# A fused two-block transformer kernel: the dense gates' layout in DRAM

## The chip, the cores and the metric

The kernel runs as one program on one core of a Trainium2 chip. The metric is the device time of the program in microseconds, as the median of several runs. The core has five engines that are named by their letters here: PE (matrix multiplication), DVE (VectorE), ACT (ScalarE), POOL (GpSimd) and SP (which issues DMAs). Sixteen DMA engines move data between DRAM and on-chip memory; they take their work from queues. In this kernel q1 is the queue of the transfers that SP issues, and q0 the queue of the gathers that POOL issues.

## The reference

One sequence of 512 tokens with 1024 features in float32 passes through two blocks. The first has a convolution branch, a windowed attention branch and then PEER, a layer with 16,384 small experts; the second has a linear recurrence, a sliding attention and a cross attention. The change is in PEER:

```
sc = einsum('thpd,pnd->thpn', q, sub_keys)      # 8 heads x 2 halves x 128 keys
vals, idx = top_k(sc, 16)
cand = vals[:, :, 0, :, None] + vals[:, :, 1, None, :]
top_s, pos = top_k(cand, 16)                     # 16 experts per head, 128 per token
gate = softmax(top_s)
u = expert_u[expert_idx];  act = gelu(einsum('thkd,td->thk', u, hc))
out = einsum('thk,thkd->td', gate * act, expert_v[expert_idx])
```

An expert's number is 128 i + j, with key i of the first half and key j of the second.

## The kernel before

The kernel handles the four tiles of 128 tokens in two ways. The two tiles of the front (`dense = 2`, 256 tokens) go through all 16,384 experts as dense matrix products, with a gate of zero where an expert was not chosen. The two other tiles fetch only their chosen experts, a row of u and v of 8 KB per token and expert: 256 gathers of 128 rows (1 MB each), issued by POOL (line 193) into six slots of `uv`. For each gather DVE makes a dot product with the token's row (L220), ACT the gelu and the scaling (L222, L223), and DVE adds the scaled v to x (L231); only then is the next gather issued. Both ways run at the same time.

The dense way has two stages. In `route` the gate matrix is built. For each block of 16 tokens (`sub`, eight per tile, so 16 in all) DVE, POOL and ACT make one-hot matrices A and B (L734, L737, L745), PE multiplies them (L747) and ACT copies the result into `cs`, 128 partitions (key i) by 128 keys j by 16 tokens, 1 MB (L749). SP writes cs into the DRAM tensor `gates` (L753). `cs` has two buffers. Beside this PE already computes the first 32 values of j of the expert activations (`expert_in`, L835 loads a tile of u of 512 KB, L837 multiplies, L839 applies gelu). The tiles of u lie in six buffers.

In `experts` the loop runs over 16 groups of eight keys j. For each group SP loads `cg`, the gates of these eight keys for all 256 tokens, 1 MB in two buffers (L853). For each pair of keys DVE multiplies the activations by cg in place (L860). Then some steps of the gathered way are put in: the remaining gathers (POOL issues 232 from 875 us on) are spread evenly over the 64 pairs, so 3 or 4 per pair. SP loads the two tiles of v (L865, 512 KB each, four buffers), PE multiplies (L869, 16 matmuls) and adds up in four banks, and `expert_in` is called for the pair that is 16 pairs later. Its result goes into the slot of `acts` that the present pair has just left, so that DVE can be at most 16 pairs ahead of PE.

The order on each engine is fixed when the program is built: a scheduler puts the instructions in order by priority and by its own costs, and the engines then wait for one another by semaphores. All loads and stores by SP leave in one order in one queue, so v and u stand behind cg where cg was issued first. A read of `gates` waits until all writes into it that it needs have landed; since each group needs all 16 blocks, the first cg waits for the last write.

In DRAM `gates` has the form [16 blocks, 128 partitions, 128 keys x 16 tokens]. A write of one block is 8 KB in a row for each partition. A read of a group takes, for each partition, 16 pieces of 512 bytes that lie 1 MB apart.

Of the kernel before, what the change touches and what calls it, by code (L numbers as in the profile page):

```python
# [8 lines left out]
F32 = mybir.dt.float32  # L9
# [231 lines left out]
class Kern:  # L241
    ahead = 32
    dense = 2
    slots = 6
    near = 6
    low = False
    wide = False

# [403 lines left out]
    def peer(self, x, h, xp):  # L652


        nc, C, tc = self.nc, self.const, self.tc
        n = self.dense * 128
        with ExitStack() as st:
            kp = st.enter_context(tc.tile_pool(name="pk", bufs=1, reuse_waits="tile"))
            self.consts(kp, ("colsp",))
            self.wide = True  # L660
            dp = st.enter_context(tc.tile_pool(name="dp", bufs=1, space=bass.MemoryType.DRAM))
            gates = dp.tile([n // 16, 128, 128 * 16], F32, name="gates")
            gp = st.enter_context(tc.tile_pool(name="gp", bufs=1, reuse_waits="tile"))
            rows = kp.tile([128, NT - self.dense, 1024], F32, name="rows")
            nc.sync.dma_start(rows, self.rowsd)
            hd = kp.tile([128, 8, n], F32, name="hd")
            nc.vector.tensor_tensor(hd, *(u[:, :, 0:n].bitcast(F32) for u in h), op=OP.add)
            got = Fetch(self, rows, x, gp)
            acts = []
            with tc.tile_pool(name="rp", bufs=2, reuse_waits="tile") as rp:  # L670
                self.low = True
                self.route(h, gates, rp, got, lambda j: self.expert_in(hd, j, acts))
                self.low = False
            with tc.tile_pool(name="ep", bufs=3, reuse_waits="tile") as ep:
                self.experts(hd, gates, x, ep, acts, got)
            with tc.tile_pool(name="fp", bufs=1, reuse_waits="tile") as fp:
                g = [self.gain(fp.tile([128, 1024], F32, name=f"g{i}"), 3 + i) for i in range(2)]
                scr = fp.tile([128, NT, 1024], F32, name="scr")
                mem = self.mem_load([[fp.tile([128, 4, 256], d, name=f"mem{i}{k}") for i in range(2)]
                                     for k, d in enumerate((F32, F32R, F32R))])  # L680
                for t in range(NT):
                    self.rms_norm(x[:, t, :], x[:, t, :], g[0], scr[:, t, :])
                    nc.sync.dma_start(self.keep[t * 128:(t + 1) * 128, :], x[:, t, :])
                self.low = True
                self.mem_values(mem, lambda: fp.tile([128, 512], F32, name="memv", bufs=2))
                self.low = False
                h = self.norm_h(x, g[1], lambda t: scr[:, t, :])
            self.wide = False
        return x, h

    def route(self, h, gates, rp, got, dense_in):
        nc, C = self.nc, self.const
        tt, cp = nc.vector.tensor_tensor, nc.vector.tensor_copy
        keys = rp.tile([128, 2, 128], F32, name="keys", bufs=1)
        nc.sync.dma_start(keys, self.ap["keys"])
        last = NT - 1
        val = rp.tile([128, last, 16, 16], F32, name="val", bufs=1)
        idx = rp.tile([128, last, 16, 16], U32, name="idx", bufs=1)
        for hp in range(16):
            ps = self.mm_t(self.ap["w_q"][hp], h)  # L700
            q = rp.tile([128, 512], F32, name="q", tag="A")
            nc.scalar.activation(q, ps, AF.Copy)
            pc = self.pa()
            for t in range(NT):
                ts = slice(t * 128, (t + 1) * 128)
                nc.tensor.matmul(pc[:, ts], q[:, ts], keys[:, hp % 2, :], start=True, stop=True)
            sc = rp.tile([128, last * 128], F32, name="sc", tag="B")
            nc.scalar.activation(sc, pc[:, 0:last * 128], AF.Copy)
            nc.scalar.activation(got.scores[:, hp, :], pc[:, last * 128:], AF.Copy)
            for t in range(last):  # L710
                self.top16(sc[:, t * 128:(t + 1) * 128], val[:, t, hp, :], idx[:, t, hp, :])
        dense_in(None)

        def select(t):
            w = got.weights(t) if t >= self.dense else rp.tile([128, 8, 16], F32, name="w")
            return self.select(rp, val[:, t], idx[:, t], w)

        for t in range(self.dense, last):
            got.choose(t, *select(t))
        got.start()  # L720
        for t in range(self.dense):
            pt = self.pa()
            for n, a in enumerate(select(t)):
                nc.tensor.transpose(pt[:, n * 128:(n + 1) * 128], a.rearrange("p a b -> p (a b)"), self.ident)
            ijw = rp.tile([128, 3, 128], F32, name="ijw", bufs=1)
            nc.scalar.activation(ijw, pt[:, :384].rearrange("p (a b) -> p a b", b=128), AF.Copy)  # L726
            for sub in range(8):
                cs = rp.tile([128, 128, 16], F32, name="cs")
                for c8 in range(2):
                    t0 = sub * 16 + c8 * 8  # L730
                    A, B = (rp.tile([128, 8, 128], F32, name=n) for n in "AB")
                    for n, o, k in ((0, A, 8), (1, B, self.near - 1)):
                        sh = [128, k, 128]
                        tt(o[:, :k], C["iota"][:, None, :].to_broadcast(sh),  # L734
                           ijw[:, n, t0:t0 + k, None].to_broadcast(sh), op=OP.is_equal)
                    for n in range(self.near - 1, 8):
                        (nc.vector if n < self.near else nc.gpsimd).tensor_scalar(  # L737
                            B[:, n, :], C["iota"], ijw[:, 1, t0 + n:t0 + n + 1], ijw[:, 2, t0 + n:t0 + n + 1],
                            op0=OP.is_equal, op1=OP.mult)
                    for c4 in range(2):  # L740
                        pg = self.pa()
                        for n in range(4):
                            i = c4 * 4 + n
                            if i < self.near - 1:
                                nc.scalar.activation(B[:, i, :], B[:, i, :], AF.Copy,  # L745
                                                     scale=ijw[:, 2, t0 + i:t0 + i + 1])
                            nc.tensor.matmul(pg[:, n * 128:(n + 1) * 128], A[:, i, :], B[:, i, :], start=True, stop=True)  # L747
                        o = c8 * 8 + c4 * 4
                        nc.scalar.activation(cs[:, :, o:o + 4].rearrange("p j t -> p t j"),  # L749
                                             pg.rearrange("p (t j) -> p t j", j=128), AF.Copy)  # L750
                    if c8:
                        got.step(1)
                nc.sync.dma_start(gates[t * 8 + sub], cs.rearrange("p j t -> p (j t)"))  # L753
                if sub % 2:
                    j = (t * 4 + sub // 2) * 2
                    if j < self.ahead:
                        dense_in(j)
        for j in range(self.dense * 8, self.ahead, 2):
            dense_in(j)
# [82 lines left out]
        p = j // 2 % 16  # L842
        return acts[p // 8][:, p % 8, :]

    def experts(self, h, gates, x, ep, acts, got, G=8):
        nc = self.nc
        n = self.dense * 128
        po = [[self.bank("pv") for half in range(2)] for t in range(self.dense)]
        left, pairs = got.left(), 64
        late = self.late_tile(got, ep)  # L850
        for g in range(128 // G):
            cg = ep.tile([128, n // 16, G, 16], F32, name="cg", bufs=2)
            nc.sync.dma_start(cg.rearrange("p s j t -> p s (j t)"),  # L853
                              gates.rearrange("s p c -> p s c")[:, :, g * G * 16:(g + 1) * G * 16])
            for jj in range(0, G, 2):
                j = g * G + jj
                a = self.slot(acts, j)
# [617 lines left out]
```

## Time and profile before

| what | value |
|---|---|
| median of 3 runs | 2588.4 us (2586.82 to 2592.43) |
| profiled execution, its own time | 2582.75 us |
| its span | 2580.9 us |
| PE busy | 2291.4 us (89%) |
| DVE busy | 1776.9 us (69%) |
| POOL busy | 722.7 us (28%) |
| data moved by DMA | 551.15 MB, mean 214 GB/s |

All times inside the program are from the profiled execution and count from the start of its span. The busy share of an engine is a mean over the whole program, whose stages have different limits: `route` builds gates from 718 to 865 us, the expert loop runs from about 875 to 1848 us. A DMA share of 1 or a little over it stands for DMA engines that are never idle.

### The profile page before, as it was taken

The numbers are of one execution on the slowest core, as the hardware profiler recorded it, in microseconds if no ns is written. First come the engines' busy times: TensorE is split into PE (matmuls) and PEld (weight loads), VectorE is DVE, ScalarE is ACT, GpSimd is POOL, SyncE is SP. The second block draws the span as 40 slices with busy tenths as digits, with TensorE's granted clock in tenths as the row PEclk, the third lists the DMA queues.
The fourth block names the chain that finished last, engine by engine and source line by source line (L and its number), as shares of the span: only waits on it lengthen the run. The fifth ranks groups of instructions, "written<-read, shape, count | busy, mean of one in ns | idle before, by whom it ended". The sixth has DMA issues, their size and how long they took to land.

```text
span 2580.9 us, 31619 instructions
## 1 busy us (share of the span) xinstructions
PE 2291.4 (89%) x11682; PEld 1664.2 (64%) x11682; DVE 1776.9 (69%) x3529; ACT 839.1 (33%) x1797; POOL 722.7 (28%) x443
## 2 busy tenths in 40 slices
PE   7999969979999769897488877999889999999999
PEld 6876748868877536464255544653467787778887
DVE  6998984456988669786666746767766676675332
ACT  4244453333286411111111111111344333564221
POOL 3532214133196534343343423433200000000000
PEclk9999979989999889898799988999989999999999
DMA  4221113332676999999989989999621001121323
GB/s 163 100 74 58 58 65 115 106 109 89 238 250 244 340 410 399 401 405 390 411 340 389 415 340 389 410 417 417 261 79 40 26 26 34 58 90 66 104 92 123
DMA packets 142522, 551.15 MB, mean 214 GB/s; under 512 B 12704, under 2 KB 47392, under 8 KB 107040
## 3 DMA queue, kind: packets, MB, share of 16 engines
q1 hardware_dynamic: 105504, 280.69, 30.5%
q0 software_dynamic: 36864, 268.45, 25.8%
q8 instruction: 92, 1.51, 0.2%
q14 instruction: 62, 0.51, 0.1%
HBM read 524.97 MB, written 24.12 MB: 213 GB/s over the span
## 4 chain that ended last, share of the span: by engine, by line
PE 39%; DMA 16%; DVE 5%; another core or an unknown queue 3%; issue 2%; ACT 1%; POOL 1%; SPq 0%; POOLq 0%; DVEq 0%; ACTq 0%
DMA v<-v 13%; PE pv L869 11%; PE ps L837 5%; PE ps L325 4%; PE ps L324 4%; PE ps L323 4%; DMA cg<-gates 2%; PE pa L325 1%; PE pa L324 1%; PE pa L323 1%; POOL uv L193 1%; DVE x L231 1%; PE pf L620 1%; PE pa L1110 1%
## 5 line engine op out<-in xcount | busy, mean ns | idle before, releaser
L193 POOL DMA_INDIRECT uv<-uv,ge x256 | 386.9, 1511 | 652.1 <-DVE x L231 516.6
L837 PE MATMUL ps<-hd,u 128*128 128x256 f32 x2048 | 464.5, 381 | 0.0
L837 PEld LDWEIGHTS ps<-hd,u 128*128 128x128 f32 x2048 | 386.6, 192 | 70.4 <-issue 20.5
L231 DVE SCALAR_TENSOR_TENSOR x<-uv,s,x 128x1024 f32<-128x1024 f32 x256 | 327.9, 1281 | 115.5 <-ACT s L223 115.5
L323 PE MATMUL ps<-hh,whi 128*128 128x512 f32 x920 | 367.7, 400 | 3.8 <-ACT u L958 1.7
L325 PE MATMUL ps<-hh,wlo 128*128 128x512 f32 x920 | 368.4, 400 | 0.4 <-POOL wlo L318 0.4
L324 PE MATMUL ps<-hl,whi 128*128 128x512 f32 x920 | 368.1, 400 | 0.0
L869 PE MATMUL pv<-v,ah 128*128 128x512 f32 x512 | 239.7, 622 | 135.5 <-DMA v<-v 129.6
L318 POOL TENSOR_TENSOR wlo<-wraw,whi 128x1024 fp32r<-128x1024 f32 x84 | 205.1, 2443 | 479.3 <-ACT whi L317 426.5
L220 DVE CUSTOM_DVE_ANT_0 uv<-uv,rows 128x1024 f32<-128x1024 f32 x256 | 317.1, 1239 | 29.5 <-DMA uv<-uv,ge 29.3
L869 PE MATMUL pv<-v,al 128*128 128x512 f32 x512 | 238.7, 616 | 47.0 <-DMA v<-v 35.7
L317 ACT ACTIVATE whi<-wraw 128x1024 fp32r<-128x1024 f32 x151 | 159.8, 1059 | 346.1 <-PE ps L324 215.3
L869 PEld LDWEIGHTS pv<-v,ah 128*128 128x128 f32 x512 | 100.6, 200 | 262.0 <-issue 191.5
L222 ACT ACTIVATE s<-s 128x1 f32<-128x1 f32 x256 | 51.7, 202 | 618.7 <-DVE s L220 618.6
L869 PEld LDWEIGHTS pv<-v,al 128*128 128x128 f32 x512 | 98.5, 197 | 174.6 <-issue 133.1
L323 PEld LDWEIGHTS ps<-hh,whi 128*128 128x128 f32 x920 | 175.2, 191 | 41.4 <-ACT u L958 2.2
L325 PEld LDWEIGHTS ps<-hh,wlo 128*128 128x128 f32 x920 | 175.1, 190 | 38.6 <-issue 2.9
L324 PEld LDWEIGHTS ps<-hl,whi 128*128 128x128 f32 x920 | 175.1, 190 | 36.8 <-issue 2.5
L533 DVE SCALAR_TENSOR_TENSOR pm<-u,cols,pm 128x512 f32<-128x512 f32 x232 | 174.6, 753 | 5.3
L318 DVE TENSOR_TENSOR wlo<-wraw,whi 128x1024 fp32r<-128x1024 f32 x67 | 81.9, 1222 | 111.3 <-ACT whi L317 110.9
L737 POOL TENSOR_SCALAR B<-colsp,ijw 128x128 f32<-128x128 f32 x64 | 109.3, 1713 | 23.8 <-ACT ijw L726 23.3
L860 DVE TENSOR_TENSOR ah<-ah,cg 128x256 f32<-128x256 f32 x64 | 25.1, 420 | 103.1 <-ACT ah L839 76.8
(499 smaller groups left out, 3398.8 us busy)
## 6 DMA issues: line engine op xcount, KB each, us to landing
u<-u SPq DMA_DIRECT2D x128, 512.0 KB, 9.1
v<-v SPq DMA_DIRECT2D x128, 512.0 KB, 11.8
wraw<-w2t SPq DMA_DIRECT2D x49, 512.0 KB, 3.4
wraw<-w1t SPq DMA_DIRECT2D x42, 512.0 KB, 3.4
gates<-cs SPq DMA_DIRECT2D x16, 1024.0 KB, 4.8
cg<-gates SPq DMA_DIRECT2D x16, 1024.0 KB, 26.2
wraw<-w_out SPq DMA_DIRECT2D x16, 512.0 KB, 3.4
wraw<-w_q SPq DMA_DIRECT2D x16, 512.0 KB, 3.5
```

The source lines that it names most:

```text
L193: self.k.nc.gpsimd.indirect_dma_start(t, None, self.k.ap["uv"], bass.IndirectOffsetOnAxis(ap=self.e[g][:, s:s + 1], axis=0))
L220: nc.vector.tensor_tensor_reduce(out=u, in0=u, in1=self.rows[:, g, :], scale=1.0, scalar=0.0, op0=OP.mult, op1=OP.add, accum_out=d)
L231: self.k.nc.vector.scalar_tensor_tensor(x, t[:, 1024:2048], c, x, op0=OP.mult, op1=OP.add)
L317: nc.scalar.activation(hi, raw, AF.Copy)
L318: (nc.gpsimd if self.low else nc.vector).tensor_tensor(lo, raw, hi.bitcast(F32), op=OP.subtract)
L323: mm(out, ah, bh, start=start, stop=False)
L324: mm(out, ah, bl, start=False, stop=False)
L325: mm(out, al, bh, start=False, stop=stop)
L533: nc.vector.scalar_tensor_tensor(acc[:, b, :] if j == 30 else part, u[:, b, j:j + 512], w[:, j:j + 1], part, op0=OP.mult, op1=OP.add)
L737: (nc.vector if n < self.near else nc.gpsimd).tensor_scalar(B[:, n, :], C["iota"], ijw[:, 1, t0 + n:t0 + n + 1], ijw[:, 2, t0 + n:t0 + n + 1],
L837: nc.tensor.matmul(ps[:, i * 256:i * 256 + 256], raw[:, k * 128:k * 128 + 128], h[:, k, :], start=k == 0, stop=k == KC - 1)
L869: nc.tensor.matmul(po[t][half], a[:, ts], v[:, half * 512:half * 512 + 512], start=j + i == 0, stop=j + i == 127)
```

## The change

The DRAM tensor gets the form [16 groups, 128 partitions, 16 blocks, 8 keys x 16 tokens], and the group size 8 becomes a field of the class. The write of one block now puts, for each partition, 16 pieces of 512 bytes 1 MB apart; the read of one group takes 8 KB in a row for each partition. The bytes, the number of DMAs and the computation are the same.

```diff
@@ class Kern
     near = 6
+    group = 8
@@ peer
-            gates = dp.tile([n // 16, 128, 128 * 16], F32, name="gates")
+            gates = dp.tile([128 // self.group, 128, n // 16, self.group * 16], F32, name="gates")
@@ route
-                nc.sync.dma_start(gates[t * 8 + sub], cs.rearrange("p j t -> p (j t)"))
+                nc.sync.dma_start(gates[:, :, t * 8 + sub, :].rearrange("g p c -> p g c"),
+                                  cs.rearrange("p (g j) t -> p g (j t)", j=self.group))
@@ experts
-    def experts(self, h, gates, x, ep, acts, got, G=8):
-        nc = self.nc
+    def experts(self, h, gates, x, ep, acts, got):
+        nc, G = self.nc, self.group
...
             cg = ep.tile([128, n // 16, G, 16], F32, name="cg", bufs=2)
-            nc.sync.dma_start(cg.rearrange("p s j t -> p s (j t)"),
-                              gates.rearrange("s p c -> p s c")[:, :, g * G * 16:(g + 1) * G * 16])
+            nc.sync.dma_start(cg.rearrange("p s j t -> p s (j t)"), gates[g])
```

## Rows read from the trace of the kernel before

**Rows 1.** The page's 40 equal slices: busy tenths of the DMA engines, and GB/s.

```profile
DMA  4221113332676999999989989999621001121323
GB/s 163 100 74 58 58 65 115 106 109 89 238 250 244 340 410 399 401 405 390 411 340 389 415 340 389 410 417 417 261 79 40 26 26 34 58 90 66 104 92 123
```

**Rows 2.** Table by stages: from:to us, length; busy us (instructions) by engine; clock, DMA share, GB/s.

```profile
801.00:865.00 64.00, 55.76 (x329) 45.71 (x328) 52.73 (x68) 53.42 (x123) 62.30 (x39) 0.98 0.74 270
...
890.00:1606.00 716.00, 557.43 (x1847) 357.60 (x1846) 495.52 (x833) 109.57 (x388) 277.00 (x175) 0.89 0.99 390
1606.00:1820.00 214.00, 205.24 (x589) 108.57 (x587) 153.87 (x193) 35.51 (x127) 83.35 (x60) 1.00 1.02 415
```

**Rows 3.** Waits of PE, 875 to 1850 us: total us, times, longest us.

```profile
PE pv L869 <- DMA v<-v: 165.3, 18, 38.1
```

**Rows 4.** Timeline of SP, PE, DVE, 1225 to 1325: start, length, instruction [idle before, releaser].

```profile
1234.54 0.38 SPq L853 DMA_DIRECT2D cg<-gates  x1
1235.01 27.53 SPq L865 DMA_DIRECT2D v<-v  x2
...
1240.71 7.07 PE L837 MATMUL ps<-hd,u 128*128 128x256 f32 x32
1285.87 8.96 PE L869 MATMUL pv<-v,ah 128*128 128x512 f32 x16 [38.09 <-DMA v<-v]
...
1302.40 0.76 DVE L860 TENSOR_TENSOR ah<-ah,cg 128x256 f32<-128x256 f32 x2 [27.16 <-ACT ah L839]
```

**Rows 5.** DMA packets and queues, 1250 to 1260: packets, MB, share of 16 engines.

```profile
DMA packets 1056, 4.09 MB, mean 409 GB/s; under 512 B 61, under 2 KB 590, under 8 KB 590
...
q0 software_dynamic: 527, 3.82, 93.1%
q1 hardware_dynamic: 529, 0.27, 9.6%
```

**Rows 6.** DMA issues, whole span: count, KB each, median us from issue to landing.

```profile
gates<-cs SPq DMA_DIRECT2D x16, 1024.0 KB, 4.8
cg<-gates SPq DMA_DIRECT2D x16, 1024.0 KB, 26.2
...
out_dram<-x SPq DMA_DIRECT2D x8, 256.0 KB, 2.0
...
kv<-pT SPq DMA_DIRECT2D x2, 256.0 KB, 2.4
```

**Rows 7.** DMA packets, 1290 to 1300 us.

```profile
DMA packets 501, 1.81 MB, mean 181 GB/s; under 512 B 60, under 2 KB 60, under 8 KB 501
```

**Rows 8.** DMA packets and an issue, 1846 to 1872 us.

```profile
DMA packets 1153, 4.20 MB, mean 162 GB/s; under 512 B 128, under 2 KB 128, under 8 KB 1152
...
mem<-memT SPq DMA_DIRECT2D x2, 512.0 KB, 4.6
```

**Rows 9.** DMA packets and queues, 1770 to 1780; then packets, 1200 to 1210.

```profile
DMA packets 767, 4.17 MB, mean 417 GB/s; under 512 B 85, under 2 KB 85, under 8 KB 431
...
q0 software_dynamic: 383, 2.75, 66.3%
q1 hardware_dynamic: 384, 1.42, 35.4%
...
DMA packets 3414, 3.52 MB, mean 352 GB/s; under 512 B 92, under 2 KB 2924, under 8 KB 3399
```

**Rows 10.** DMA packets, 880 to 1820 us.

```profile
DMA packets 96965, 371.43 MB, mean 395 GB/s; under 512 B 7358, under 2 KB 40046, under 8 KB 67334
```

**Rows 11.** Timeline, 855 to 900 us (gathers: first and last of five); chain, 700 to 905.

```profile
863.06 1.45 POOL L193 DMA_INDIRECT uv<-uv,ge  x1 [0.17 <-issue]
...
873.21 0.94 POOL L193 DMA_INDIRECT uv<-uv,ge  x1 [4.25 <-DVE x L231]
...
887.86 1.43 DVE L860 TENSOR_TENSOR ah<-ah,cg 128x256 f32<-128x256 f32 x4 [14.93 <-DMA cg<-gates]
...
864.85 9.91 DMA gates<-cs
```

## The prediction, made before the change was run

> **What bounds the kernel now.** I read the 40 slices first. The reader is to see a stretch of thirteen slices (about 840 to 1,810 us) in which the core's DMA moves 340 to 417 GB/s, while everywhere else it moves far less [rows 1]. This is the expert loop. The table by stages says the same: from 890 to 1606 us the DMA share is 0.99 at 390 GB/s and PE works 557 of 716 us; from 1606 to 1820 us the share is 1.02 at 415 GB/s [rows 2]. The waits of PE in the loop come next: 165.3 us for tiles of v, in 18 waits of up to 38.1 us [rows 3]. A DMA that ran evenly would cause many short waits, not 18 long ones, so I looked for what makes them long.
>
> The timeline around one of them shows it [rows 4]. SP issues a load of cg at 1234.54 and v right behind it, at 1235.01. PE ends its matmuls of u at 1247.8 and then stands for 38.09 us until the v arrives. What the queues did meanwhile is in the 10 us from 1250 [rows 5]: the gathers' queue (q0) sent 527 packets with 3.82 MB, SP's queue (q1) 529 packets with 0.27 MB. So the two queues take turns packet by packet; a packet of cg is 512 bytes, one of a gather is 7 to 8 KB, and SP's queue gets 7% of the bytes for as long as cg is in it. The cg loads land 26.2 us after issue at the median [rows 6], and v and u behind them in the same queue are as late. The gathers meanwhile run far ahead, until VectorE stands too, 27.16 us at 1302.40, for an activation that PE has not fed [rows 4]. Then the gathers have no free slots and PE has its backlog of v, and the DMA falls to 181 GB/s [rows 7].
>
> **Part 1: cg becomes contiguous.** With the new layout gates[g] is 8 KB in a row per partition on both sides. That such a view is really sent as one run is seen at the two loads of memT, whose views have two inner dimensions (4 x 256) as well: in their stretch the packets under 2 KB are the 128 that are under 512 B, so no 1 KB pieces were sent, which would have been 1,024 more [rows 8]. So a cg load is 128 packets instead of 2,048.
>
> The service time: from 1770 to 1780 us, with no cg in the queues, 4.17 MB took 10 us, 2.40 us per MB [rows 9]. From 1200 to 1210 us there were 2924 - 92 = 2832 pieces of 512 B, 1.45 MB, among 3.52 MB [rows 9]. The other 2.07 MB at 2.40 are 4.97 us, so the small ones took 5.03 us, 3.47 us per MB. A cg of 1.05 MB costs 3.64 us of all DMA engines now and 2.52 after; sixteen of them save 18.0 us.
>
> The Trainium skill, "DMA: Bandwidth & Descriptors", section "Specifications", puts the smallest transfer for line rate at 512 B. By that rule cg is at full rate already and this term is nothing: the sum below would come to about 2568 instead of 2550. The trace differs (3.47 against 2.40 us per MB), and I go by the trace.
>
> The idle time: from 880 to 1820 us 371.43 MB were moved, of which 40046 - 7358 = 32,688 pieces of 512 B are 16.74 MB [rows 10]. 354.69 MB x 2.40 + 16.74 MB x 3.47 = 851 + 58 = 909 us of 940. The DMA stood 31 us in sum. This is what follows the starving of SP's queue. After the change cg's 8 packets per engine alternate with gather packets of the same size, so cg delays v by twice 2.52 us and not by 26, and the gathers can't run ahead during it. Bounds: all 31 us go, or none (the gathers still have larger packets than v and u: 66.3% against 35.4% of the engines when both queues are full [rows 9], and so may run ahead without cg's help). I take 25 us. The stretch from 1606 us, with one cg at its start, shows 415 GB/s with nothing lost [rows 2], which is why I go near the upper end; the 6 us that I leave are for the dips that no cg explains.
>
> What is late next is still the DMA: 673 us for the stretch 890 to 1606 are left, against 557 us of PE work and 496 us of DVE [rows 2]. So no engine is reached. Loop in all: -43 us.
>
> **Part 2: the writes of cs become scattered.** Each of the 16 writes is now 2,048 pieces of 512 B instead of 128 of 8 KB. SP's issue is no dearer than that of cg now (0.38 us [rows 4]). Service time, by the read price: 1.05 MB x (3.47 - 2.40) = 1.1 us more each. By writes: a 256 KB store of pT into kv, whose runs are 512 B, lands after 2.4 us, a 256 KB store of the output after 2.0 us [rows 6]; four times the difference is 1.6 us. So 18 to 26 us for all 16. What hides it: in 801 to 865 us POOL works 62.3 of 64 us and the DMA share is 0.74 [rows 2]. One step of eight takes 8 us there; the DMA is busy 5.9 us of it, 7.0 to 7.5 after. The write is not waited for either: cs has two buffers, so a write has about 8 us before ACT needs its buffer back, and now lands after 4.8 [rows 6]. Behind it in SP's queue wait the u loads into six buffers. A gather in flight holds the write up by its own 2.5 us. I take 2 us of the bound 0 to 26; if the cover were gone it would be all 26.
>
> The Trainium skill, "DMA: Bandwidth & Descriptors", section "Latency and other measured facts", speaks against this part: copies between HBM tensors fell from 207 GB/s at a row pitch of 512 KiB to 164 at 2 MiB, and here a partition's 16 pieces lie 1 MiB apart. As an estimate from that page a write would take 5.7 us, over the 4.6 us that rival B allows, and the time would be about 2567. The cg reads of before walk the same addresses and take 3.64 us, so I don't take it.
>
> **Part 3: the hand-over.** The first cg waits for the last write; SP stands at it, with v behind. Before: write issued at 864.85, landed 9.91 us later, first multiply by cg at 887.86 [rows 11]. In that time POOL issues five gathers, at 863.06 to 873.21 [rows 11]. After: while they last the write gets one small packet per gather packet. Five gathers are 5.24 MB, at the packet size of rows 5 some 720 packets, 45 per engine; of the write's 128 per engine 45 go beside them. 5.24 MB x 2.40 + 0.37 MB x 3.47 = 13.9 us, the other 0.68 MB 2.4 us, and about 1.4 us to completion (256 KB land in 2.0 us, less 0.6 of moving): 17.7 us, 7.8 more. Then cg comes alone, since DVE stands and all slots are full: 2.5 + 1.4 = 3.9 us instead of 13.0, so 9.1 less. The DMA stands some 3 us more in this. I take +2; bounds -4 and +8.
>
> **Sum.** -18 - 25 + 2 + 2 = -39 us. The profiled execution took 2582.75 us (span 2580.9), so 2544; the median of the three timed runs is 5.65 us above it, so 2549.4, and I say 2550. This case's own range: 2535 to 2566 (the idle term at -31 or -14, the writes at 0 or +6, the hand-over at -4 or +4).
>
> **Rivals.**
> A. Only the service time is saved. The gathers still run ahead by their larger packets, DVE reaches its limit of sixteen pairs ahead as before, and the 31 us of standing DMA stay. -18 + 4: 2574. For it: the 2:1 shares of rows 9. Against: with cg out of the queue the DMA is full at these shares, and once DVE is at its limit the gathers only follow PE.
> B. The writes become the bound of the routing stage, and the kernel is slower. A step has 8 us and 3.4 us of other DMA work (5.9 - 2.5), so a write that needs over 4.6 us of the engines makes the DMA the bound in place of POOL. The loop's gain of about 40 us over 16 writes is 2.5 us each, so from 7.1 us per write it is slower than before; at 8.5 us it is 16 x 3.9 - 40 = +22: 2610. For it: no write of this size in 512 B pieces is in the trace. Against: both nearest rows say 3.6 to 4.1 us.
> C. It does not do what it says: cg is still sent in 512 B pieces, as the call still names three dimensions. Then only the costs are left, +4 to +8: 2594. Against: rows 8.
>
> **How the numbers follow.** What a measurement of this kernel can tell from no change is about 0.2%, 5 us. Forecast 0.68 and A 0.18 are faster; B 0.08 is slower; C 0.04 is half no change, half slower; 0.02 is left for a loss elsewhere that just cancels the gain. Faster 0.86, same 0.04, slower 0.10. The range must hold 0.8: all of the forecast's, and most of A, 2534 to 2577.
>
> **What would show it.** Step 1 right: packets under 2 KB in the loop near 7,400 instead of 40,046, cg landing in 5 to 10 us, no 10 us in which q0 has over 3.5 MB and q1 under 0.4, and the loop about 40 us shorter at 410 GB/s or more. If the rate while both queues are full is 417 but stretches like rows 7 remain, A holds. Step 2 right: gates landing at 5 to 7 us, the stage 718 to 865 us not over 3 us longer, POOL still at 97% of it; if DMA is at 1.0 there with POOL standing, B holds. Step 3: first multiply by cg 20 to 29 us after the last write's issue. The prediction is wrong if PE's waits for v in the loop don't fall by about 35 us, or if another stage than these changes by more than 3 us.

## The result, and the profile after the change

The changed kernel takes 2548.0 us (median of four runs, 2544.0 to 2549.4) against 2590.41 us for the kernel before, measured beside it (2586.82 to 2593.49). The ratio is 0.9849, with a 95% interval of 0.9812 to 0.9887; measured again later it was 0.9854 (0.9809 to 0.9898). So it is 1.5% faster, about 39 us (29 to 49 by the interval). The profiled executions differ by 35.0 us in span (2580.9 and 2545.9).

The page's 40 slices after the change (first the busy tenths of the DMA engines, then GB/s) answer to [rows 1]:

```profile
DMA  4321213332667999999999999999411010122323
GB/s 165 102 75 50 67 50 124 116 103 84 240 216 254 306 412 417 417 417 418 417 417 417 417 418 417 417 417 404 161 64 34 27 35 27 59 100 67 100 92 123
```

Where the expert loop went up and down between 340 and 417 GB/s, it now holds 417 in every slice but the first and the last. The same in the table by stages (busy us of PE, PEld, DVE, ACT, POOL, then clock, DMA share, GB/s), beside [rows 2]; the first line is the routing stage:

```profile
717.00:865.00 148.00, 134.19 (x766) 111.00 (x765) 126.46 (x224) 111.33 (x254) 121.11 (x73) 0.99 0.81 257
...
890.00:1562.00 672.00, 591.94 (x1908) 368.95 (x1909) 509.22 (x838) 108.51 (x390) 183.86 (x175) 0.94 1.02 417
1562.00:1780.00 218.00, 197.64 (x547) 101.94 (x545) 150.45 (x190) 34.57 (x126) 59.09 (x58) 0.98 1.01 413
```

The routing stage of the kernel before, in the same 148 us:

```profile
717.00:865.00 148.00, 134.38 (x769) 111.43 (x770) 127.78 (x225) 111.68 (x252) 121.14 (x74) 0.99 0.73 259
```

POOL, PE, DVE and ACT do the same work in it as before; only the DMA share went from 0.73 to 0.81. That is 11.8 us of busy DMA time, about 0.8 us for each of the 15 scattered writes that fall in it (the last one is issued at its end), and no time of the kernel.

Packets of the changed kernel, 880 to 1780 us, beside [rows 10]:

```profile
DMA packets 67069, 373.09 MB, mean 415 GB/s; under 512 B 7415, under 2 KB 7815, under 8 KB 35335
...
q0 software_dynamic: 33352, 242.86, 65.3%
q1 hardware_dynamic: 33675, 129.72, 35.8%
```

And its packets and queues in the same 10 us as in [rows 5] (packets, MB, share of 16 engines):

```profile
DMA packets 761, 4.19 MB, mean 419 GB/s; under 512 B 80, under 2 KB 80, under 8 KB 419
...
q0 software_dynamic: 383, 2.80, 67.4%
q1 hardware_dynamic: 378, 1.39, 34.7%
```

The 32,688 pieces of [rows 10] have shrunk to 400 (at the edge of the window, from the last write). The same 371 to 373 MB pass in 900 us and not in 940. The queues still take turns packet by packet (383 and 378 in the 10 us, 33,352 and 33,675 in the 900), but SP's queue now sends 4 KB or 8 KB in its turn (rows of v and u, rows of cg), and so gets about a third of the bytes.

Waits of PE and of DVE in the loop after the change (total us, times, longest), beside [rows 3]:

```profile
PE pv L870 <- DMA v<-v: 112.7, 34, 19.0
...
DVE uv L220 <- DMA uv<-uv,ge: 143.6, 206, 3.0
```

The same wait of DVE in the kernel before:

```profile
DVE uv L220 <- DMA uv<-uv,ge: 28.5, 37, 2.0
```

PE's waits for v fell by 53 us and became short ones: two long ones are left, the first (14.6 us, at the hand-over) and the longest (19.0 us, at the loop's end, below), and none between them is over 6.7 us. DVE now waits for almost every gather: the gathers no longer get the whole DMA for 40 us at a time, and the chain of waits that ends last runs through them.

One thing looks worse. Median us from issue to landing, after the change, beside [rows 6]:

```profile
u<-u SPq DMA_DIRECT2D x128, 512.0 KB, 25.4
v<-v SPq DMA_DIRECT2D x128, 512.0 KB, 24.8
...
gates<-cs SPq DMA_DIRECT2D x16, 1024.0 KB, 6.1
cg<-gates SPq DMA_DIRECT2D x16, 1024.0 KB, 18.4
```

and of v in the kernel before:

```profile
v<-v SPq DMA_DIRECT2D x128, 512.0 KB, 11.8
```

A load of v took 11.8 us at the median before and takes 24.8 now. The equal numbers of packets over the 900 us say that both queues hardly ever ran empty, so each load stands behind others. A longer way to landing is no loss where the DMA is full all the time.

SP's own instructions for the loads of v show one thing more, which the prediction does not name (min/median/max ns, first and last start; before, then after):

```profile
L865 SPq DMA_DIRECT2D v<-v x128: 327/328/34772, 875.3 to 1834.7; - x128
...
L866 SPq DMA_DIRECT2D v<-v x128: 327/328/697, 884.9 to 1799.5; - x128
```

Before, a load of v behind a load of cg could hold SP for 20 to 35 us in its issue (the 27.53 us for two loads of v in [rows 4] are such a case); after, none takes over 0.70 us. So v was late not only because it stood behind cg in the queue, but also because its own issue took so long. The runs do not part these two.

### The profile page after: what moved, and what is told of

Same layout as the page of the kernel before. It is cut to its first block, busy times and chain, and to the rows that moved or that the text cites. A ratio compares the mean times of both kernels' runs of the same rounds, so it can differ in the third digit from the quotient of the medians.

```text
span 2545.9 us, 31619 instructions
## 1 busy us (share of the span) xinstructions
PE 2308.1 (91%) x11682; PEld 1663.3 (65%) x11682; DVE 1791.0 (70%) x3529; ACT 837.6 (33%) x1797; POOL 609.0 (24%) x443
## 4 chain that ended last, share of the span: by engine, by line
DMA 27%; PE 24%; DVE 7%; issue 5%; ACT 2%; POOL 2%; SPq 0%; POOLq 0%; DVEq 0%; ACTq 0%
DMA uv<-uv,ge 26%; PE ps L326 5%; PE ps L324 4%; PE ps L325 4%; DVE x L231 2%; PE pa L326 1%; PE pa L325 1%; PE pa L324 1%; POOL uv L193 1%; DMA gates<-cs 1%; PE pf L621 1%; PE pa L1105 1%; POOL B L738 1%; PE pf L648 1%; PE pa L1111 1%
## 5 line engine op out<-in xcount | busy, mean ns | idle before, releaser
L193 POOL DMA_INDIRECT uv<-uv,ge x256 | 272.6, 1065 | 734.3 <-DVE x L231 585.1
L870 PE MATMUL pv<-v,ah 128*128 128x512 f32 x512 | 246.0, 633 | 67.6 <-DMA v<-v 55.8
L870 PE MATMUL pv<-v,al 128*128 128x512 f32 x512 | 248.7, 635 | 63.1 <-DMA v<-v 56.9
L748 PE MATMUL pv<-B,A 128*128 128x128 f32 x512 | 82.3, 297 | 14.5 <-POOL B L738 11.1
## 6 DMA issues: line engine op xcount, KB each, us to landing
v<-v SPq DMA_DIRECT2D x128, 512.0 KB, 24.8
cg<-gates SPq DMA_DIRECT2D x16, 1024.0 KB, 18.4
```

What stands on the lines that cost most here:

```text
L193: self.k.nc.gpsimd.indirect_dma_start(t, None, self.k.ap["uv"], bass.IndirectOffsetOnAxis(ap=self.e[g][:, s:s + 1], axis=0))
L870: nc.tensor.matmul(po[t][half], a[:, ts], v[:, half * 512:half * 512 + 512], start=j + i == 0, stop=j + i == 127)
```

## The experiments

**The reads in pieces again, the writes as after.** A gap of 512 bytes behind each piece keeps the new layout and the order of the instructions on every engine, but a read of cg can't be sent as one run.

```diff
-gates = dp.tile([128 // self.group, 128, n // 16, self.group * 16], F32, name="gates")
+gates = dp.tile([128 // self.group, 128, n // 16, self.group * 32], F32, name="gates")
...
-nc.sync.dma_start(gates[:, :, t * 8 + sub, :].rearrange("g p c -> p g c"),
+nc.sync.dma_start(gates[:, :, t * 8 + sub, 0:self.group * 16].rearrange("g p c -> p g c"),
...
-nc.sync.dma_start(cg.rearrange("p s j t -> p s (j t)"), gates[g])
+nc.sync.dma_start(cg.rearrange("p s j t -> p s (j t)"), gates[g][:, :, 0:G * 16])
```

> The new layout with a gap of 512 bytes behind every piece, so that the reads of cg are 512 B pieces again while the writes stay scattered and the order on every engine stays as it is. My theory (the gain lies in the packets of the cg reads alone, 18 us of service and some 30 us of standing DMA; the writes cost about nothing): the gain is gone, 2588 to 2598 us, v waits of PE in the loop at 150 us or more in long waits, cg landing at 20 us or more. Rival (where the data lie in DRAM, or the stage of the writes, gave the gain): it stays at 2545 to 2560.

Measured: 2596.69 us, 1.005 of the kernel before (1.0024 to 1.0075); the profiled execution was the shortest of its ten, 2575.76 us. PE's waits in the loop, and the packets of 890 to 1780 us:

```profile
PE pv L870 <- DMA v<-v: 151.7, 17, 36.4
...
DMA packets 91858, 353.47 MB, mean 397 GB/s; under 512 B 6994, under 2 KB 37714, under 8 KB 63591
```

The gain is gone, and 17 long waits are back, with the data in the new places and the writes scattered. So it comes from the packets of the cg reads. (The pieces of a write now lie 2 MiB apart; the routing stage takes 147 us with them, as before.) The +0.5% that is left would fit the scattered writes with nothing to pay for them; it was not taken apart.

**Rows on both sides.** The old layout with each group reading one block's rows.

```diff
-gates.rearrange("s p c -> p s c")[:, :, g * G * 16:(g + 1) * G * 16])
+gates[15 - g].rearrange("p (s c) -> p s c", c=G * 16))
```

> The old layout written in 8 KB rows, and the reads in 8 KB rows too: each group reads one block's rows instead of its own keys, so the gates that it multiplies by are the wrong ones; the work is the same. It is the changed kernel without the scattered writes. My theory: the writes cost only at the hand-over, where the last one landed after 20.4 us instead of 9.9; so 2 to 8 us faster than the changed kernel, 2540 to 2546 us, the last write landing after about 10 us, and the first multiply by cg about 15 to 18 us after its issue instead of 25. Rival B (the writes slow the routing stage): the stage from 718 to 864 us gets shorter by over 5 us.

Measured: 2541.63 us, 0.9835 (0.9791 to 0.9879), 6 us under the changed kernel, which the interval does not tell from nothing; the trace does. Its chain at the hand-over, the first multiply by cg, and the first and last matmul of pv:

```profile
861.81 9.87 DMA gates<-cs
...
880.84 1.43 DVE L860 TENSOR_TENSOR ah<-ah,cg 128x256 f32<-128x256 f32 x4 [9.94 <-DMA cg<-gates]
...
884.73 7.75 PE L869 MATMUL pv<-v,ah 128*128 128x512 f32 x13 [10.23 <-DVE x L231]
...
L869 PE MATMUL pv<-v,al x512: 592/592/1193, 995.1 to 1808.0; 128*128 128x512 f32 x171
```

The last write lands after 9.87 us, as before the change, and the first multiply starts 19.0 us after its issue instead of 25.3, a little over the 15 to 18 that I expected. From the first to the last matmul of pv it is 923.8 us, as in the changed kernel, so in the loop the two are alike and the writes cost only at the hand-over. The routing stage (first write at 716.8, last at 861.8) is 145 us long against 146.7: the scattered writes don't slow it by more than 2 us. Rival B is not there with one write per block.

**The blocks broken up, the pieces kept.** cg is read in four parts, one behind the v loads of each pair, a group ahead (`issue_after` puts what is issued in its block behind the given instruction of the same engine).

```diff
+def part(c, g, i):
+    s = slice(4 * i, 4 * i + 4)
+    nc.sync.dma_start(c[:, s].rearrange("p s j t -> p s (j t)"),
+                      gates[s].rearrange("s p c -> p s c")[:, :, g * G * 16:(g + 1) * G * 16])
...
+if nxt is not None:
+    with self.tc.issue_after(at.ins):     # at: the last v load of the pair
+        part(nxt, g + 1, jj // 2)
```

> The old layout, but each cg is read in four parts of 256 KB (still pieces of 512 B), one part behind the v loads of each pair, a group ahead. The bytes and the packets are those of the kernel before; only the long blocks of 2,048 packets in SP's queue are broken up. If the standing DMA came from the long blocks: 2588 - 15 to -25 us, so 2563 to 2573, with PE's longest wait for v at 15 us or less, and the service of small pieces still at about 3.5 us per MB. Rival (it is the number of turns that SP's queue needs, however they are spread): 2583 to 2595.

Measured: 2566.46 us, 0.992 (0.9898 to 0.9942). Its waits and packets (890 to 1780 us):

```profile
PE pv L877 <- DMA v<-v: 157.5, 23, 13.0
...
DMA packets 91859, 358.54 MB, mean 403 GB/s; under 512 B 7767, under 2 KB 36951, under 8 KB 62927
```

The 29,184 small pieces (36951 - 7767) are 14.94 MB. At the prices of the prediction they and the rest need 51.8 + 824.6 = 876 us of 890, so the DMA stood 14 us where it had stood 31 in [rows 10]'s 940 (and 31 in these 890 too). PE's waits for v hardly fell in sum (157.5 us against 165.3), but none is over 13.0 us. With the same bytes and the same packets, breaking up the blocks and moving the parts behind the loads of v gave about 20 us (15 to 26 by the interval). The rival, that only the number of turns counts, falls. What the order alone is worth beside small pieces was not run; the next run shows that it is worth nothing beside large ones.

**The same parts in rows of 2 KB.** The new layout, with the same order on every engine as in the run before.

```diff
-    nc.sync.dma_start(c[:, s].rearrange("p s j t -> p s (j t)"),
-                      gates[s].rearrange("s p c -> p s c")[:, :, g * G * 16:(g + 1) * G * 16])
+    nc.sync.dma_start(c[:, s].rearrange("p s j t -> p s (j t)"), gates[g][:, s])
```

> The same four parts at the same places and the same order on every engine as in the run with parts in the old layout, but in the new layout, so that a part is 2 KB in a row per partition. Between the two only the size of the pieces differs (512 B read or written). My theory: the DMA is full all through the loop as in the changed kernel, 2545 to 2552 us; the distance to the run with parts in the old layout is then the service time of the small pieces, 18 us, and what is left of the blocking. Rival (the order of the issues matters and not the packets): both runs with parts are within 5 us of each other.

Measured: 2549.02 us, 0.9851 (0.9806 to 0.9896), 17.4 us less than with small pieces, and what the changed kernel takes with its undivided loads. Waits and packets:

```profile
PE pv L878 <- DMA v<-v: 108.9, 36, 13.2
...
DMA packets 71698, 366.68 MB, mean 412 GB/s; under 512 B 7954, under 2 KB 7954, under 8 KB 42190
```

At 2.40 us per MB its bytes need 880 us of the 890: the DMA stood 10 us, not none as I expected, and 14 in the run before. So the two terms were taken apart, if roughly: about 20 us for the long blocks, and 17 us for the small pieces, of which some 4 are standing DMA. The writes differ too (scattered only here), but the way from the last write's issue to the first matmul of pv is 25 us in both.

**Every block written twice.** A second write, to a spare tensor, tests the bound of rival B.

```diff
+self.spare = dp.tile([128 // self.group, 128, n // 16, self.group * 16], F32, name="spare")
...
-nc.sync.dma_start(gates[:, :, t * 8 + sub, :].rearrange("g p c -> p g c"),
-                  cs.rearrange("p (g j) t -> p g (j t)", j=self.group))
+for to in (self.spare, gates):
+    nc.sync.dma_start(to[:, :, t * 8 + sub, :].rearrange("g p c -> p g c"),
+                      cs.rearrange("p (g j) t -> p g (j t)", j=self.group))
```

> The changed kernel, but every block of cs is written twice in 512 B pieces, once into a spare tensor that nobody reads. The loop reads what it read. By the bound that rival B gave (a step of 8 us holds 3.4 us of other DMA work, so 4.6 us for writes), two writes of 3.6 us are over it: the steps go from 8 to 10.5 us or more, so the stage from 717 to 864 us gets 30 to 45 us longer, its DMA share goes to 0.95 or more and POOL falls below 85%: 2578 to 2595 us. If instead POOL hides the writes whatever they cost, the stage stays at 147 us and the time at 2548 to 2556.

Measured: 2589.84 us, 1.0017 (0.9992 to 1.0043). Table of 717 to 865 us, its issues, and SP's instructions for the second write (min/median/max ns, first and last start):

```profile
717.00:865.00 148.00, 115.04 (x653) 97.98 (x653) 115.40 (x210) 96.93 (x221) 106.56 (x65) 0.91 0.98 305
...
gates<-cs SPq DMA_DIRECT2D x16, 1024.0 KB, 12.5
cg<-gates SPq DMA_DIRECT2D x16, 1024.0 KB, 15.5
...
L756 SPq DMA_DIRECT2D gates<-cs x16: 1834/3976/15775, 719.1 to 883.7; - x16
```

The DMA is full (0.98) and POOL has fallen from 121 to 107 us. The first cg is issued at 914.1 us instead of 884.5, 30 us later: the last write is issued at 883.7 instead of 864.0, and lands after 30 us instead of 20. With 0.8 us more than the 2.52 of a row write, a scattered one is 3.3 us, and two of them and 3.4 us of other work would be 10 us for a step of 8. The steps came to 8.9 to 9.6 us, since part of the other work moved behind the stage (11 loads of u were issued in it instead of 18). SP was held up as well: it took 4.0 us at the median to issue the second write and 15.8 us for the last, where a write of the changed kernel takes 0.36. So the cover that the prediction counted on is real and has an edge between one such write and two; how much of the delay is the DMA engines' time and how much SP's issue was not taken apart. (The order on all engines differs from the changed kernel's here, so the 12 us that the rest lost can't be put down to one thing.)

**Half the bytes.** Gates in float16.

```diff
-gates = dp.tile([...], F32, name="gates")
+gates = dp.tile([...], F16, name="gates")
...
-cs = rp.tile([128, 128, 16], F32, name="cs")
+cs = rp.tile([128, 128, 16], F16, name="cs")
...
-cg = ep.tile([128, n // 16, G, 16], F32, name="cg", bufs=2)
+cg = ep.tile([128, n // 16, G, 16], F16, name="cg", bufs=2)
```

> The changed kernel with the gates kept as float16 in cs, DRAM and cg (their values are rounded), so that cg is half the bytes: 8.4 MB less are read in the loop, in rows of 4 KB, and the writes go in pieces of 256 B. My theory (the loop is now bound by the bytes that DMA moves, 2.40 us per MB): 20 us less, 2524 to 2532 us, with the loop still at 415 GB/s or more. Rival (PE or the gathers' chain through DVE has become the bound): less than 8 us, 2540 to 2548, with the loop's rate falling below 412 GB/s.

Measured: 2584.78 us, 1.0001 (0.9974 to 1.0028): neither. ACT's copies into cs in the changed kernel and here (min/median/max ns, first and last start), and 717 to 865 us here:

```profile
L750 ACT ACTIVATE cs<-pv x64: 1015/1062/1110, 710.7 to 863.0; 128x512 f32<-128x512 f32 x64
...
L750 ACT ACTIVATE cs<-pv x64: 2311/2367/2715, 714.7 to 932.8; 128x512 f16<-128x512 f32 x64
...
717.00:865.00 148.00, 106.04 (x549) 87.52 (x550) 89.85 (x178) 122.31 (x171) 83.94 (x51) 0.92 0.48 148
```

The copy took 2.37 us, where the changed kernel's takes 1.06; 64 of them made ACT the bound of the routing stage, and the last write left at 935.5 us, 71 us late. From the first cg on, the run was 17 us shorter than the changed kernel (1644 us against 1661). I had looked only at the loop.

**Half the bytes, the copy turned**, and the same turn in float32 as a control:

```diff
-nc.scalar.activation(cs[:, :, o:o + 4].rearrange("p j t -> p t j"),
-                     pg.rearrange("p (t j) -> p t j", j=128), AF.Copy)
+nc.scalar.activation(cs[:, :, o:o + 4],
+                     pg.rearrange("p (t j) -> p j t", j=128), AF.Copy)
```

> The float16 gates again (rounded), but ACT copies the bank into cs with the token innermost, so that four float16 values lie side by side for each key, where the run before wrote single ones 32 bytes apart and took 2.37 us per copy instead of 1.06. My theory now: the loop did get shorter by the bytes saved (from the first cg's issue to the end 1644 us against 1661), and only the slower copy by ACT cost the routing stage 70 us; with a copy of 1.1 us or less the whole is 2526 to 2534 us. If float16 output itself is slow on ACT at this size, the copy stays over 2 us and the time at 2575 to 2590.

> The changed kernel in float32 with only the order of the copy turned (token innermost). Control for the float16 run: if the order alone makes the copy shorter or longer than 1.06 us it shows here. ACT is not the bound of the routing stage (111 of 148 us), so 2543 to 2552 us if the copy is at 1.1 us or less; over 1.4 us it becomes the bound (64 copies) and the time goes up by 10 us or more.

Measured: 2526.59 us in float16, 0.9783 (0.9737 to 0.9829), and 2545.19 us in float32, 0.9843 (0.9799 to 0.9888). The copies in float16, and its packets of 890 to 1562 us:

```profile
L750 ACT ACTIVATE cs<-pv x64: 576/597/599, 713.5 to 866.6; 128x512 f16<-128x512 f32 x64
...
DMA packets 51119, 279.95 MB, mean 417 GB/s; under 512 B 5668, under 2 KB 5668, under 8 KB 28259
```

and in float32:

```profile
L750 ACT ACTIVATE cs<-pv x64: 576/597/599, 712.9 to 866.6; 128x512 f32<-128x512 f32 x64
...
DMA packets 50011, 279.89 MB, mean 417 GB/s; under 512 B 5543, under 2 KB 5543, under 8 KB 26181
```

Both copies take 0.60 us. In float32 that is worth nothing that can be told, since POOL bounds the stage. In float16 it sets the loop's gain free: 18.6 us between these two runs, where 8.4 MB at 2.40 us are 20. Not all of it is the loop's: the traces put some 6 us at the hand-over (the first matmul of pv at 887.9 us against 894.2) and some 16 in the loop, where 15 of the 16 loads of cg fall. In both the DMA moves 417 GB/s all through, so the loop is bound by the bytes that the DMA moves.

The changed kernel beside these two:

> The changed kernel itself, beside the two on the same chip: 2544 to 2550 us, ratio to the kernel before 0.981 to 0.989.

It took 2547.44 us.

**The loop's end.** The timeline of PE at the end of the loop, in the kernel before:

```profile
1832.77 15.70 PE L869 MATMUL pv<-v,al 128*128 128x512 f32 x32 [2.91 <-DMA v<-v]
```

and in the changed kernel, then its table of 1790 to 1800 us, and SP's longest waits of 1740 to 1815 us:

```profile
1792.42 5.88 PE L870 MATMUL pv<-v,al 128*128 128x512 f32 x8 [19.01 <-DMA v<-v]
1802.32 12.23 PE L870 MATMUL pv<-v,al 128*128 128x512 f32 x24 [4.02 <-DVE rows L1223]
...
1790.00:1800.00 10.00, 5.88 (x8) 2.25 (x8) 7.80 (x11) 2.78 (x7) 0.00 (x0) 0.66 0.12 27
...
SPq L314 <- POOL wlo L319: 25.0, 2, 23.1
...
SPq L283 <- DVE s L220: 13.5, 1, 13.5
```

The same two waits of SP in the kernel before, 1780 to 1850 us:

```profile
SPq L282 <- DVE s L220: 14.0, 1, 14.0
...
SPq L313 <- POOL wlo L318: 1.1, 1, 1.1
```

SP stands at loads for the next stages (w_mem at L314, consts3 at L283) with the last loads of v behind them. The wait at consts3 was there before; the one at w_mem has grown from 1.1 to 25.0 us. I put these loads behind the last v (`issue_after` around `mem_values`, and around the loads of consts3 and pos), in the changed kernel and in the float16 version.

> The changed kernel, with the loads for the stages after the loop (w_mem, consts3, pos) put behind the last v in SP's queue. In the changed kernel SP stands at a w_mem load for a buffer that POOL holds (25 us of waits) and at consts3 for the last gather (13.5 us), both with v loads behind them, and PE then waits 19 us for v at 1792 while the DMA share falls to 0.12. Before the change PE came there later and the same wait cost it 2.9 us. If this is what the loop's end lost: 6 to 15 us less, 2532 to 2541 us, with the last matmul of pv at 1806 or earlier instead of 1814. If the w_mem loads are needed as early as they were, the gain comes back behind the loop: 2543 to 2550.

> The same turn of the order on the float16 version (rounded gates) that ran 2526.6 us. If the two gains are independent: 2511 to 2521 us. If the float16 loop's end doesn't have the stall in that size: 2522 to 2528.

Measured: 2538.07 us, 0.9805 (0.9787 to 0.9824), and 2520.59 us, 0.9751 (0.9732 to 0.9769). The first is 9 to 10 us under the changed kernel, and none of its five runs (2533.89 to 2539.54) reaches the lowest of that one's eight (2544.0). In float16 the step is 6 us, and the intervals (0.9737 to 0.9829 without it) do not tell it from nothing. PE in the first of them:

```profile
1739.88 48.93 PE L871 MATMUL pv<-v,al 128*128 128x512 f32 x104
1817.17 0.80 PE L324 MATMUL ps<-whi,mem 128*128 128x512 f32 x1 [28.36 <-ACT mem L341]
```

The matmuls of pv now end at 1788.8 instead of 1814.6, 26 us earlier, and PE then waits 28.4 us for the split of mem; 9 us of the 26 are left at the end. This one in float32 is the fastest of these versions that computes with the same precision, the float16 one the fastest of all.

## Why the prediction was right

The forecast was 2550 us and -39 us; measured were 2548.0 and about -39. That the two agree so closely is in part luck: the interval is 29 to 49 us, the profiled executions differ by 35.0, and the loop gained 8 us less than forecast. The mechanism came as told, but for the time that SP itself spent on issuing v, which the prediction does not name. By its steps:

- **Service time of cg, -18.** Right, as far as the runs can tell: 17.4 us between the two runs with parts, of which some 4 are standing DMA. The price itself holds over the whole loop: a fit over the windows of 10 us from 890 to 1800 us in which the DMA share is 1 or more (81 of 91) gives 2.40 us per MB and 3.4 for the pieces of 512 B, beside the 3.47 that I took from one window.
- **Standing DMA, -25 of 31.** Right in kind: with the blocks broken up and their parts behind v, the run was about 20 us shorter and the DMA stood 14 us. In size the DMA did better than I took: 373.09 MB at 2.40 are 895 of 900 us, so only 5 are left, and those at the window's edges. The DMA has moved the loop's 371 to 373 MB by 1780 instead of 1820 us, 40 earlier, with the first multiply by cg 1.5 us later.
- **What was not in the sum: the loop's end.** From the first to the last matmul of pv it is 35.4 us less (959.2 to 923.8), not 43. While the DMA is through with the loop's bytes 40 us earlier, pv ends only 34 earlier. Before, PE had work of its own left and met SP's stalled queue with a wait of 2.9 us; now it waits 19. "What is late next" should have been asked of the last pairs too. The run with v first shows the place.
- **The writes, +2 of 0 to 26.** Right: the stage is 146.7 us long against 146.3, so even the 2 us were too many. The price per write was at or below both rows that I took it from (1.1 and 1.6 us more): 0.8 us more by busy share, and 1.0 by the same fit over the full windows of the run with doubled writes (12 of 19 from 717 to 907 us; 3.4 us per MB, give or take 0.2).
- **The hand-over, +2.** Right: the write landed after 20.36 us (17.7 forecast) and cg after 4.83 (3.9), as the chain and timeline show, beside [rows 11]:

```profile
864.03 20.36 DMA gates<-cs
884.51 4.83 DMA cg<-gates
...
889.36 1.43 DVE L861 TENSOR_TENSOR ah<-ah,cg 128x256 f32<-128x256 f32 x4 [15.15 <-DMA cg<-gates]
890.73 2.05 PE L870 MATMUL pv<-v,ah 128*128 128x512 f32 x2 [14.62 <-DMA v<-v]
```

  and the first matmul of pv in the kernel before:

```profile
889.25 11.02 PE L869 MATMUL pv<-v,ah 128*128 128x512 f32 x20 [12.06 <-DMA v<-v]
```

  From the write's issue to the first matmul of pv it was 24.4 us and is 26.7.
- **A sign that I gave and that was wrong:** cg landing in 5 to 10 us, with v held up by twice 2.52. It lands after 18.4, v after 24.8, as the two queues hardly ever ran empty. The gain did not need it: the DMA is full all the same.
- **A count that was wrong:** the stretch from 840 to 1,810 us in [rows 1] has fifteen slices, not thirteen. Nothing in the sum rests on it.

Of the rivals, A (the 2:1 shares let the gathers run ahead) is refuted by 417 GB/s all through the loop at shares of 67.4% and 34.7%. B is refuted at this size of write, and the doubled writes show where it would begin. C is refuted by the packets. Of the two rules of the Trainium skill, "DMA: Bandwidth & Descriptors", the smallest transfer for line rate (section "Specifications") does not hold for 512 B pieces here: they take 3.4 us per MB against 2.40, and the two runs with parts differ by 17.4 us. The slowing at large row pitches (section "Latency and other measured facts") was an estimate of 5.7 us per write; the traces give 3.3 to 3.6 with pieces 1 MiB apart.

## What to carry to other kernels

Where two DMA queues are busy, look at the size of the packets in each: here a queue with 512 B in its turn, beside one with 7 to 8 KB, got 7% of the bytes, and all that stood behind in its order waited. When one side of a DRAM buffer must be in small pieces, put them into the stage where the DMA has room and nobody waits. After a gain in a loop, look at its last rounds: a fixed order of issues that was covered by the old lateness may hold up the new one.

## What the runs showed of the hardware that I had not expected

- A copy by ACT of 128 x 512 from PSUM takes 1.06 us into float32 values 64 bytes apart, 2.37 us into float16 values 32 bytes apart, and 0.60 us in either type when it writes four neighbours at a time (and reads PSUM with 512 bytes from one value to the next).
- 512 B pieces cost about 3.4 us per MB, against 2.40 for rows of 4 or 8 KB, when read from DRAM (the fit over the kernel before). Written, they cost about the same: 3.2 by busy share in a stage whose DMA was not full, 3.4 with the doubled writes. That reading and writing differ is not shown.
- A DMA of 2,048 pieces can hold up the issue of the next one: a load of v right behind a cg of the kernel before held SP for up to 34.8 us, and the second of two scattered writes for 4.0 us at the median, where 0.33 and 0.36 us are the medians of v loads and single writes.
